# A row-wise top-10 kernel: reordering the extractions, masks and batches of the last tiles

## The chip, the cores and the metric

The kernel runs on one core of a Trainium2 chip. The metric is device time in microseconds (us); the span of a profile is 1.8 us shorter than the time of the same execution (692.61 and 690.8, 690.82 and 689.0). All executions told of here are of the fast state. The engines are called PE (TensorE), VectorE (DVE in the profile), ScalarE (ACT), GpSimd (POOL) and SyncE (SP, which issues the loads). "Pass" is one matmul instruction as the profile counts them: an fp32 matmul shows as two.

## The reference

```python
def setup_inputs():
    return {"x": np.random.randn(8192, 8192).astype(np.float32), "k": 10}

def reference(x, k):
    indices = np.argpartition(x, -k, axis=1)[:, -k:]
    values = np.take_along_axis(x, indices, axis=1)
    sorted_idx = np.argsort(-values, axis=1)
    return np.take_along_axis(indices, sorted_idx, axis=1)
```

## The kernel before

The 8192 rows are 64 tiles of 128 rows. A row is cut into 8 parts, so that a tile holds each row on 8 partitions. Per tile: ScalarE takes steep exponentials; PE sums them over groups of eight columns ("weigh"); VectorE finds the best 16 of the 1024 sums ("choose") and writes the indices of 12 of them; GpSimd gathers the elements behind these ("gather"); VectorE and GpSimd multiply them with a mask, half each ("spread"); PE brings the 96 candidates of each row together in 12 small fp32 matmuls ("extract"); VectorE ranks them ("rank"). Every eight tiles "finish" turns positions into column numbers: seven VectorE steps (slot, low, hot, hot, pick, val, rows), one PE matmul for each tile ("move"), a cast and an output transfer that is issued from ScalarE's queue. Three tiles are loaded ahead.

```python
    starts = list(range(0, ntiles, TB)) + [last - 2, last]      # TB = 8, last = 63
    # ... (cut)
    def spread(t):
        masked[t] = small.tile([P, G, P // 16, 16], fp32, tag="masked", name="masked")
        cand = cands.pop(t)
        half = G // 2                                           # G = 12
        shape = [P, half, P // 16, 16]
        for eng, g0 in ((nc.vector, 0), (nc.gpsimd, half)):
            eng.tensor_tensor(out=masked[t][:, g0:g0 + half], # ... (cut)
                              op=ALU.mult)

    def extract(t):
        mk = masked.pop(t)
        gs[t] = gpsum.tile([P, G, R], fp32, tag="g", name="g")
        for c in range(G):
            nc.tensor.matmul(gs[t][:, c, :], lhsT=mk[:, c, :, :].rearrange("p a s -> p (a s)"),
                             rhs=place, start=True, stop=True)
    # ... (cut)
        for t in range(last):
            interleave(choose_steps(t), rank_steps(t - LAG) if t >= LAG else [])   # LAG = 3
            if t >= 1:
                spread(t - 1)
            gather(t)
            weigh(t + 1)
            if t >= 1:
                extract(t - 1)
            todo = 3 if t < last - 1 else len(later)
            run(later[:todo])                                   # steps of a finished batch
            later = later[todo:]
            # ... (cut: a finished batch appends its finish steps to later; load(t + 3))
        run(choose_steps(last))
        gather(last)
        # ... (cut: a test of the sums, "good")
        spread(last - 1)
        extract(last - 1)
        run(rank_steps(last - 3))
        run(rank_steps(last - 2))
        steps = finish_steps(batch_of[last - 3])
        run(steps[:-2])
        spread(last)
        extract(last)
        run(rank_steps(last - 1))
        run(steps[-2:])
        # ... (cut: finish of tiles 61 and 62, rank of tile 63, finish of tile 63, final test)
```

## Time and profile before

| what | before |
|---|---|
| time, median of all 4 runs known after the prediction | 695.92 us (693.69 to 696.28) |
| profiled execution: time, span | 692.61, 690.8 us |
| loads end | about 645 us |
| last choose starts, its indices are ready | 659.99, 666.46 us |
| last gather ends | 672.28 us |
| last extraction on PE | 679.58 to 682.79 us |

A row of the timeline view gives the start in us, the duration in us, engine, line and operation, the output and inputs, a count, and in brackets how long the engine had been idle and what ended the wait. "issue" there means that nothing in the profile explains the wait. The column after the counts in the view by stretches is the granted share of PE's clock, then the share of the DMA engines and GB/s. One thing in the table will matter below: the profiled execution was faster than any of the four timed ones. The prediction took its durations from that one execution. It was not a freak: of the 41 runs of before in the three groups of experiments below, 12 took under 694 us, 25 over 695.3 and only 4 lie between.

### The profile page before, as it was taken

How to read it: one execution, taken by the hardware profiler on the slowest of the kernel's cores; microseconds unless marked ns; L12 is line 12 of the kernel's file. 1: busy time of each engine (PE TensorE's matmuls, PEld its weight loads, DVE VectorE, ACT ScalarE, POOL GpSimd, SP SyncE). 2: the span in 40 equal slices, each digit the busy share in tenths (PEclk: the TensorE clock that was granted, in tenths of full speed). 3: DMA queues.
4: the chain of work that ended last, by engine and by line, in shares of the span. 5: the costliest groups of instructions: out<-in, count | busy, mean ns of one | idle time of the engine just before them, and what ended most of it. 6: DMA issues, size and time to landing. Idle time of an engine off the chain costs nothing.

```text
span 690.8 us, 7979 instructions
## 1 busy us (share of the span) xinstructions
PE 551.9 (80%) x2690; PEld 340.2 (49%) x2690; DVE 562.6 (81%) x1322; ACT 489.0 (71%) x264; POOL 180.9 (26%) x135
## 2 busy tenths in 40 slices
PE   1587977798898888888987888787987888887835
PEld 0153544464554455555644545554553555654434
DVE  1577787888978997798878898869977897879876
ACT  4777777777777777777777777677777767777700
POOL 0113322322331332232233133313322313332211
PEclk9876688768866688777888698859887677788875
DMA  8999999999999999999999999999999999999300
GB/s 348 421 421 420 419 421 419 421 420 421 419 421 420 419 420 419 421 419 421 420 419 420 419 421 420 420 420 421 415 419 421 420 420 420 421 420 421 140 5 6
DMA packets 70604, 269.69 MB, mean 390 GB/s; under 512 B 4386, under 2 KB 5026, under 8 KB 70562
## 3 DMA queue, kind: packets, MB, share of 16 engines
q1 hardware_dynamic: 69760, 268.45, 94.9%
q10 hardware_dynamic: 802, 0.73, 0.3%
q8 instruction: 21, 0.34, 0.2%
q14 instruction: 21, 0.17, 0.1%
HBM read 268.51 MB, written 0.66 MB: 390 GB/s over the span
## 4 chain that ended last, share of the span: by engine, by line
DMA 56%; PE 12%; DVE 11%; issue 7%; ACT 6%; SPq 5%; POOL 2%; ACTq 0%; POOLq 0%
DMA xt<-in_x_dram 53%; PE s L152 8%; ACT e L144 6%; SPq L94 5%; DMA out_dram<-opack 3%; PE g L212 3%; DVE wall L171 3%; POOL cand L185 2%; DVE m L172 1%; DVE cidb L176 1%; DVE cidb L174 1%; DVE wall L175 1%; DVE masked L201 1%; PE fo L250 1%; DVE pick L267 0%
## 5 line engine op out<-in xcount | busy, mean ns | idle before, releaser
L144 ACT ACTIVATE e<-xt,bias 128x4096 bf16<-128x4096 f32 (+2 forms) x131 | 475.5, 3630 | 157.1 <-DMA xt<-in_x_dram 143.5
L152 PE MATMUL s<-e,group 128*128 128x512 bf16 x1024 | 342.2, 497 | 120.1 <-ACT e L144 119.9
L152 PEld LDWEIGHTS <-group 128*128 128x128 bf16 x1024 | 122.6, 123 | 312.3 <-issue 256.5
L212 PEld LDWEIGHTS g<-cpack,masked 128*128 128x128 f32 x1536 | 208.1, 215 | 29.4 <-issue 15.7
L212 PE MATMUL g<-cpack,masked 128*128 128x8 f32 x1536 | 200.1, 269 | 12.3 <-DVE masked L201 8.5
L185 POOL INDIRECT_COPY cand<-xt,idx 128x192 f32 x64 | 64.5, 1007 | 489.1 <-DVE t8a L223 141.5
L171 DVE MAX8 wall<-s 128x8 f32<-128x1024 f32 x64 | 78.8, 1232 | 113.0 <-PE s L152 112.8
L201 POOL TENSOR_TENSOR masked<-cand,cpack 128x768 f32<-128x768 f32 x64 | 115.5, 1806 | 5.2
L174 DVE FIND_INDEX8 cidb<-wall,s 128x8 uint16<-128x1024 f32 x64 | 78.3, 1223 | 0.0
L176 DVE FIND_INDEX8 cidb<-wall,m 128x8 uint16<-128x1024 f32 x64 | 78.0, 1219 | 0.0
L172 DVE MATCH_REPLACE8 m<-wall,s 128x1024 f32<-128x1024 f32 x64 | 77.7, 1214 | 0.0
L175 DVE MAX8 wall<-m 128x8 f32<-128x1024 f32 x64 | 77.3, 1208 | 0.0
L201 DVE TENSOR_TENSOR masked<-cand,cpack 128x768 f32<-128x768 f32 x64 | 60.7, 949 | 0.0
L250 PE MATMUL fo<-rows,send 128*64 128x160 f32 (+3 forms) x128 | 26.2, 347 | 2.7 <-DVE rows L270 2.7
L144 ACT ACTIVATION_READ_ACCUMULATOR e<-xt,bias 128x1 f32 x131 | 24.4, 186 | 0.0
L330 ACT ACTIVATE e<-tall,bias 128x64 f32<-128x64 f32 x1 | 0.3, 348 | 29.6 <-DVE tall L229 29.6
L250 PEld LDWEIGHTS fo<-rows,send 128*64 128x64 f32 (+3 forms) x128 | 16.8, 146 | 4.5 <-issue 3.0
L223 DVE MAX8 t8a<-g 128x8 f32<-128x96 f32 x64 | 15.9, 248 | 0.8 <-PE g L212 0.8
L226 DVE FIND_INDEX8 posb<-t8a,g 128x8 uint16<-128x96 f32 x64 | 16.4, 256 | 0.0
L228 DVE FIND_INDEX8 posb<-t8b,g 128x8 uint16<-128x96 f32 x64 | 16.1, 252 | 0.0
L224 DVE MATCH_REPLACE8 g<-t8a,g 128x96 f32<-128x96 f32 x64 | 15.9, 248 | 0.0
L227 DVE MAX8 t8b<-g 128x8 f32<-128x96 f32 x64 | 15.5, 243 | 0.0
(37 smaller groups left out, 107.6 us busy)
## 6 DMA issues: line engine op xcount, KB each, us to landing
xt<-in_x_dram SPq DMA_DIRECT2D x248, 1024.0 KB, 16.4
xt<-in_x_dram SPq DMA_DIRECT2D x16, 512.0 KB, 9.5
out_dram<-opack ACTq DMA_DIRECT2D x7, 80.0 KB, 5.2
cpack<-topk_cpack ACTq DMA_DIRECT2D x1, 68.5 KB
out_dram<-opack ACTq DMA_DIRECT2D x1, 50.0 KB
out_dram<-opack ACTq DMA_DIRECT2D x1, 20.0 KB, 1.5
out_dram<-opack ACTq DMA_DIRECT2D x1, 10.0 KB
```

What stands on the lines that cost most here:

```text
L94: nc.sync.dma_start(out=dst[:, s:s + n, :], in_=src[:, s:s + n, :])
L144: nc.scalar.activation(out=e[:, 0:n, :].rearrange("p s j -> p (s j)"), in_=xts[t][:, s0 * W:(s0 + n) * W], func=ACTF.Exp, bias=bias[:, 0:1 ...
L152: nc.tensor.matmul(ss[t][:, j:j + BANK], lhsT=group[:, s0 + i, :], rhs=e[:, i, j:j + BANK], start=s0 + i == 0, stop=s0 + i == S - 1)
L171: lambda: nc.vector.max(out=w16[:, 0:8], in_=m),
L172: lambda: nc.vector.match_replace(out=m2, in_to_replace=w16[:, 0:8], in_values=m, imm_value=-1.0),
L174: lambda: nc.vector.max_index(out=cid[:, 0:8], in_max=w16[:, 0:8], in_values=m),
L175: lambda: nc.vector.max(out=w16[:, 8:16], in_=m2),
L176: lambda: nc.vector.max_index(out=cid[:, 8:16], in_max=w16[:, 8:16], in_values=m2),
L185: nc.gpsimd.add_instruction(mybir.InstIndirectCopy(name=nc.get_next_instruction_name(), ins=[nc.gpsimd.lower_ap(xts[t]), nc.gpsimd.lower_a ...
L201: eng.tensor_tensor(out=masked[t][:, g0:g0 + half], in0=cand[:, g0:g0 + half].unsqueeze(2).to_broadcast(shape), in1=own.rearrange("p (c s) ...
L212: nc.tensor.matmul(gs[t][:, c, :], lhsT=mk[:, c, :, :].rearrange("p a s -> p (a s)"), rhs=place, start=True, stop=True)
L250: nc.tensor.matmul(fo, lhsT=send[:, i, 0:n * S], rhs=rows[:, i].rearrange("p a k -> p (a k)"), start=i == 0, stop=i == n - 1)
```

## The change

Its intent is to shorten the drain behind the last load: the sums of tile 63 go ahead of two extractions on PE, batch 6 (counted from 0: tiles 48 to 55) is finished sooner, the last gather follows tile 62's mask on GpSimd, the last two batches (two tiles and one) become one of three, and the masks of tiles 61 and 63 are divided anew (none and eight of twelve groups on VectorE).

```diff
@@ -78,7 +78,7 @@
 
     last = ntiles - 1
 
-    starts = list(range(0, ntiles, TB)) + [last - 2, last]
+    starts = list(range(0, ntiles, TB)) + [last - 2]
     sizes = [b - a for a, b in zip(starts, starts[1:] + [ntiles])]
     batch_of = {t: b for b, t0 in enumerate(starts) for t in range(t0, t0 + sizes[b])}
 
@@ -192,15 +192,17 @@
         )
         del xts[t], idxs[t]
 
-    def spread(t):
+
+    def spread(t, ndve=G // 2):
         masked[t] = small.tile([P, G, P // 16, 16], fp32, tag="masked", name="masked")
         cand = cands.pop(t)
-        half = G // 2
-        shape = [P, half, P // 16, 16]
-        for eng, g0 in ((nc.vector, 0), (nc.gpsimd, half)):
+        for eng, g0, g1 in ((nc.vector, 0, ndve), (nc.gpsimd, ndve, G)):
+            if g0 == g1:
+                continue
+            shape = [P, g1 - g0, P // 16, 16]
             eng.tensor_tensor(
-                out=masked[t][:, g0:g0 + half],
-                in0=cand[:, g0:g0 + half].unsqueeze(2).to_broadcast(shape),
+                out=masked[t][:, g0:g1],
+                in0=cand[:, g0:g1].unsqueeze(2).to_broadcast(shape),
                 in1=own.rearrange("p (c s) -> p c s", s=16).unsqueeze(1).to_broadcast(shape),
                 op=ALU.mult,
             )
@@ -294,12 +296,12 @@
         for t in range(last):
             interleave(choose_steps(t), rank_steps(t - LAG) if t >= LAG else [])
             if t >= 1:
-                spread(t - 1)
+                spread(t - 1, 0 if t == last - 1 else G // 2)
             gather(t)
             weigh(t + 1)
-            if t >= 1:
+            if 1 <= t < last - 2:
                 extract(t - 1)
-            todo = 3 if t < last - 1 else len(later)
+            todo = 3 if t < last - 4 else 6
             run(later[:todo])
             later = later[todo:]
             done = t - LAG
@@ -307,28 +309,29 @@
                 later += finish_steps(batch_of[done])
             if t + 3 < ntiles:
                 load(t + 3)
+        extract(last - 3)
+        extract(last - 2)
         run(choose_steps(last))
+        spread(last - 1)
         gather(last)
+        extract(last - 1)
+        run(rank_steps(last - 3))
+        run(rank_steps(last - 2))
         nc.vector.tensor_scalar(
             out=good[:, 0:nsums], in0=eall, scalar1=FINITE, scalar2=None, op0=ALU.is_lt,
         )
-        spread(last - 1)
-        extract(last - 1)
-        run(rank_steps(last - 3))
-        run(rank_steps(last - 2))
         steps = finish_steps(batch_of[last - 3])
-        run(steps[:-2])
-        spread(last)
+        run(steps[:3])
+        spread(last, 8)
         extract(last)
+        run(steps[3:7])
         run(rank_steps(last - 1))
+        run(steps[7:-2])
+        run(rank_steps(last))
         run(steps[-2:])
-        steps = finish_steps(batch_of[last - 1])
-        run(steps[:-2])
-        run(rank_steps(last))
 
 
         nc.scalar.activation(out=e10, in_=tall, func=ACTF.Exp, bias=bias[:, 0:1], scale=BETA)
-        run(steps[-2:])
         run(finish_steps(batch_of[last]))
         nc.vector.scalar_tensor_tensor(
             out=good[:, nsums:nsums + ntiles], in0=e10, scalar=SLACK, in1=wall[:, :, G],
```

## The prediction

> **What bounds the kernel now.** I read the page first, its row of DMA shares in particular, then the busy times by stretch, then the chain that ended last from 640 us on, then each engine in order of time in the last 50 us. "Tile 63" is the last of 64; "choose" is the two MAX8/FIND_INDEX8 rounds on a tile's 1024 sums, "weigh" its exponentials and summing matmuls, "spread" the mask product, "extract" the 24 small matmul passes, "rank" the top 10 of 96 candidates, "finish" the assembling and storing of a batch.
>
> ```profile
> DMA 8999999999999999999999999999999999999300
> ...
> 0.00:560.00 560.00, 455.20 (x2194) 276.59 (x2195) 454.62 (x1055) 416.22 (x220) 148.66 (x113) 0.77 1.02 418
> ...
> 650.00:660.00 10.00, 9.63 (x53) 6.24 (x52) 4.96 (x14) 3.15 (x6) 2.59 (x2) 0.85 0.01 2
> 660.00:670.00 10.00, 2.39 (x12) 2.42 (x12) 9.76 (x29) 0.00 (x0) 0.00 (x0) 0.67 0.03 8
> ```
>
> Up to about 645 us the loads fill the queues (share 1.02, 418 GB/s); 268.45 MB at 420 GB/s is 639 us. Nothing in the change touches that stretch before tile 59. What can move is the drain of 690.8 - 645 = 46 us, and there the engines take turns. The start of the drain, in order of time:
>
> ```profile
> 644.53 0.19 ACT L144 ACTIVATION_READ_ACCUMULATOR e<-xt,bias 128x1 f32 x1
> 644.62 1.99 ACT L144 ACTIVATE e<-xt,bias 128x2048 bf16<-128x2048 f32 x1
> ...
> 651.96 1.15 ACT L144 ACTIVATE e<-xt,bias 128x1024 bf16<-128x1024 f32 x1 [1.28 <-issue]
> ...
> 655.20 2.74 PE L212 MATMUL g<-cpack,masked 128*128 128x8 f32 x24
> 657.87 1.84 PE L250 MATMUL fo<-rows,send 128*64 128x160 f32 x12
> ...
> 659.75 0.32 DVE L274 CAST opack<-fo 64x160 uint32<-64x160 f32 x1 [5.04 <-PE fo L250]
> 659.99 1.22 DVE L171 MAX8 wall<-s 128x8 f32<-128x1024 f32 x1
> ```
>
> Tile 63's sums are done at 655.36, yet its choose starts at 659.99: VectorE waits 5.04 us for a copy of batch 6, whose moves (12 passes) queue on PE behind an extraction (24 passes). So 4.6 us are lost to order. The rest:
>
> ```profile
> 666.23 0.23 DVE L177 TENSOR_SCALAR idx<-cidb,cpack 128x12 uint16<-128x12 uint16 x1
> ...
> 671.63 0.65 POOL L185 INDIRECT_COPY cand<-xt,idx 128x192 f32 x1 [12.54 <-issue]
> 672.25 3.55 POOL L201 TENSOR_TENSOR masked<-cand,cpack 128x768 f32<-128x768 f32 x2
> ...
> 672.42 1.70 DVE L268 SCALAR_TENSOR_TENSOR val<-low,pick 128x50 f32<-128x50 uint16 x1
> ...
> 674.15 2.50 DVE L270 TENSOR_TENSOR rows<-val,cpack 128x800 f32<-128x800 f32 x1
> ```
>
> Indices are ready at 666.46, the gather ends at 672.28, GpSimd then makes two half masks (tile 62's waited behind tile 63's gather), and VectorE's two product steps stretch: val ends at 674.12 as the first mask ends at 674.05; rows ends 0.85 us after the second. After that come extract 63 (to 682.8), rank 63 (to 684.3), a cast, finish of a batch of one tile (684.4 to 687.2), and the check (to 688.30); 2.5 us of closing end the span.
>
> **What the skill says.** "SBUF — State Buffer", section "SBUF: two separate sides": GpSimd and a VectorE operation with two SBUF inputs share a port pair, held as an exclusive lock for a whole instruction. The trace agrees: 1.70 and 2.50 us above. The gather too: its record starts 4.29 us after the indices in most tiles, 3.64 in tile 0, which no mask product follows, and 5.24, 4.86 or 5.69 in tiles where a batch's compare, multiply or spreading (1.16, 0.65, 1.48 us, two SBUF inputs each) follows. "TensorE: Matmul & The Clock Gate", section "Architectural detail: the array is 16× 32×32, not 1× 128×128": ScalarE and VectorE are strict FIFO. The trace agrees: at 271 us an exponential waited 2.34 us behind the issue of an output transfer, which waited for VectorE's cast; it began 1.0 us after that cast's start. The same page, section "The HAM clock gate": an idle PE drops to half clock. Here 12 passes took 2.70 us after an idle stretch and 24 took 2.74 when busy.
>
> **The change, part by part.** The order of instructions built from both kernels gives the moves.
>
> (1) Batch 6 is finished earlier: six of its VectorE steps run after tile 59's choose, not three and three. That adds 0.65 + 1.15 + 0.24, about 2.0 us, ahead of choose 60 (now 627.3, was 625.92, where it waited 0.64 anyway). Its spreading (1.48 us) moves ahead of choose 61, which starts 0.7 us late (636.6). Five moves then precede tile 62's sums, three follow them.
>
> (2) The cost that I find in that: the cast and the output issue of batch 6 now stand ahead of tile 63's exponentials on ScalarE (before: behind). Tile 62's sums end at 646.66; three moves are 6 passes, about 1.1 us (12 took 1.84, 4 took 0.89); cast at 647.8; ScalarE free 1.0 us later, at 648.8, not 644.62. Five exponentials with no stall: 3 x 1.99, then 1.24, and 1.29 to the start of the last sums: 657.3; 0.6 for two matmuls: 657.9. VectorE is ready earlier: choose 62 from 648.1, 7.1 us as before (646.69 to 653.79), tile 61's mask no longer on it (0.95 saved): 655.3. So choose 63 starts at 657.9, 2.1 us sooner, not the 4.6 that the removed wait promises.
>
> (3) Choose 63 takes 6.47 us (659.99 to 666.46): 664.4. GpSimd meanwhile makes all of tile 61's mask (2 x 1.8 us, from 649) and half of tile 62's (waits for extract 60, 657.9 + 2.74 = 660.7; done 662.5), so its queue is empty and the gather runs by its lead. Two tiles' ranks, the check of sums and a 0.78 us compare fall into the lead, which then spans 5.5 us to the gather's end (5.82 before with two such products): 670.0, against 672.28.
>
> (4) From gather's end G on. Mask 63 is split 8:4. VectorE 1024 elements: [...]1.22; GpSimd 512: about 1.25 (1.8 for 768). Released together on one lock, they go one after the other: G + 2.5. Then multiply, sum, val, rows: 0.51 + 0.81 + 0.20 + 0.93 = 2.45, G + 4.95 (no GpSimd in the way now). Rank 62: 1.35, G + 6.3. Extract 63: G + 2.5 + 3.2 = G + 5.7, hidden. Rank 63: 1.4, G + 7.7. Ten passes of moves after extract: G + 5.7 + 2.2 = G + 7.9; cast, 0.23. Finish of three tiles: the steps took 1.61 us for one and 2.09 for two, so 2.57: G + 10.7. Six passes and their drain 1.3: G + 12.0. Check 1.4 (686.90 to 688.30), closing 2.5: G + 15.9. Before it was 690.8 - 672.28 = 18.5, so 2.6 saved: two masks at once blocked VectorE, and there was one finish more.
>
> Sum: G falls 2.3, the rest 2.6: 4.9 us, or a span of 685.9. With the runs' 696.25: 691.3.
>
> **Rivals.** (a) ScalarE is not held by the output issue; choose 63 starts at 655.3 and the time is 688.7. For: the engine has idle time there. Against: the 2.34 us at 271 us and FIFO order. (b) The new ScalarE stall, a cold PE in the moves or extractions (2.74 becomes 5.1, as at 596 us) and the lock eat all: each costs 1 to 2.5 us; together 694 to 696. Against: most extractions lie beside choose 63; only extract 63 and the last moves are exposed. (c) The earlier burst on VectorE delays gather 59 by 0.6 us and so the last load. Its transfers queue for 12 to 16 us behind others, so it is hidden; if not, up to 1 us, 692. (d) Mask 63's VectorE part gets the lock first, and extract 63 begins on eight groups while GpSimd works: 0.5 to 1 us better, 690.5.
>
> **Range and chances.** I choose 691.2, between the sum and (d). The range 689.0 to 693.4 takes in (d) and half of (a) below, one cold stretch or a longer ScalarE stall above. Two per cent is 13.9 us, a third of the whole drain; no rival reaches it.
>
> **What would show it.** Right: ScalarE idle about 4 us before the exponentials of tile 63, ended by VectorE's cast; choose 63 near 658; no 5 us wait before the cast; last gather ending near 670; VectorE's and GpSimd's last masks end to end, one of them stretched; three closing batches become two. Wrong: exponentials going on at 644.6; loads ending later than 645; rank 63 waiting long for PE; closing longer than 2.5 us.

## The result, and the profile after

The changed kernel took 690.16 us (689.3 to 690.82), against 695.92 us before: 5.8 us less by the medians. Ratios here are the mean time of one kernel's fast runs over that of the other's of the same rounds, so not quite the ratio of the medians: 0.9923 (95% interval 0.9898 to 0.9948), "same" at the limit of 2%; of 695 us this ratio is about 5.4 us.

By stretches, the kernel after (columns as before):

```profile
DMA  9999999999999999999999999999999999999400
...
0.00:560.00 560.00, 462.11 (x2197) 285.99 (x2198) 454.63 (x1055) 416.70 (x220) 149.19 (x113) 0.76 1.02 418
...
650.00:660.00 10.00, 6.94 (x30) 3.34 (x29) 7.35 (x19) 8.08 (x10) 4.02 (x3) 0.83 0.04 9
660.00:670.00 10.00, 9.54 (x54) 9.44 (x53) 9.61 (x31) 0.00 (x0) 2.51 (x2) 0.59 0.00 0
670.00:680.00 10.00, 9.36 (x42) 8.36 (x41) 7.31 (x23) 0.00 (x0) 2.98 (x2) 0.50 0.01 2
```

The loads run as before. From 660 to 670 us PE is busy for 9.54 us instead of 2.39: the queue of extractions stands there now, beside the last choose. In spite of that its clock is 0.59 and then 0.50.

The start of the drain after, in order of time:

```profile
640.62 2.93 PE L252 MATMUL fo<-rows,send 128*64 128x160 f32 x10
...
643.48 4.27 PE L152 MATMUL s<-e,group 128*128 128x512 bf16 x16
...
644.11 0.19 ACT L144 ACTIVATION_READ_ACCUMULATOR e<-xt,bias 128x1 f32 x1
...
647.68 1.03 PE L252 MATMUL fo<-rows,send 128*64 128x160 f32 x6
...
648.74 0.32 DVE L276 CAST opack<-fo 64x160 uint32<-64x160 f32 x1 [2.86 <-PE fo L252]
...
649.10 0.47 ACTq L278 DMA_DIRECT2D out_dram<-opack  x1
649.75 2.00 ACT L144 ACTIVATE e<-xt,bias 128x2048 bf16<-128x2048 f32 x1 [5.45 <-DVE opack L276]
...
658.13 0.59 PE L152 MATMUL s<-e,group 128*128 128x512 bf16 x2 [0.54 <-ACT e L144]
...
658.76 1.23 DVE L171 MAX8 wall<-s 128x8 f32<-128x1024 f32 x1 [2.64 <-PE s L152]
```

The wait before the cast has shrunk from 5.04 to 2.86 us and no longer stands in front of the last choose. ScalarE, which had gone straight on at 644.62, now stands still for 5.45 us until the cast. The cast waits for PE, which works without a pause here: five moves of batch 6 (2.93 us, at a clock of 0.52 from 640 to 645 us), tile 62's sums to 647.75, the last three moves. So the last choose starts only 1.2 us sooner than in the profile before (658.76 for 659.99).

Around the last gather, after:

```profile
665.09 0.23 DVE L177 TENSOR_SCALAR idx<-cidb,cpack 128x12 uint16<-128x12 uint16 x1
...
670.08 0.68 POOL L185 INDIRECT_COPY cand<-xt,idx 128x192 f32 x1 [6.83 <-DVE hot L263]
...
670.79 1.23 DVE L203 TENSOR_TENSOR masked<-cand,cpack 128x1024 f32<-128x1024 f32 x1 [0.88 <-POOL cand L185]
670.84 2.29 POOL L203 TENSOR_TENSOR masked<-cand,cpack 128x512 f32<-128x512 f32 x1
671.94 1.53 DVE L266 TENSOR_TENSOR hot<-hot,cidb 128x600 f16<-128x600 f16 x1
...
672.17 5.26 PE L214 MATMUL g<-cpack,masked 128*128 128x8 f32 x24 [0.65 <-DVE masked L203]
677.36 2.89 PE L252 MATMUL fo<-rows,send 128*40 128x160 f32 x10
```

VectorE had the port pair first (1.23 us, unhindered), GpSimd's third (four groups of twelve) took 2.29 us instead of some 1.2, and VectorE's next product waited for it in turn (1.53 us for a step that took 0.47 before). The extraction behind took 5.26 us where the profile before has 3.21.

### The profile page after: what moved, and what is told of

Same layout as the page of the kernel before. It is cut to its first block, busy times and chain, and to the rows that moved or that the text cites. A ratio compares the mean times of both kernels' runs of the same rounds, so it can differ in the third digit from the quotient of the medians.

```text
span 689.0 us, 7967 instructions
## 1 busy us (share of the span) xinstructions
PE 566.8 (82%) x2690; PEld 354.3 (51%) x2690; DVE 558.5 (81%) x1313; ACT 488.8 (71%) x264; POOL 183.1 (27%) x135
## 5 line engine op out<-in xcount | busy, mean ns | idle before, releaser
L214 PEld LDWEIGHTS g<-cpack,masked 128*128 128x128 f32 x1536 | 221.3, 227 | 21.7 <-DVE masked L203 7.2
L214 PE MATMUL g<-cpack,masked 128*128 128x8 f32 x1536 | 213.0, 278 | 4.6 <-DVE masked L203 4.6
L203 POOL TENSOR_TENSOR masked<-cand,cpack 128x768 f32<-128x768 f32 x64 | 117.7, 1839 | 6.0 <-PE g L214 0.7
L203 DVE TENSOR_TENSOR masked<-cand,cpack 128x768 f32<-128x768 f32 (+1 forms) x63 | 60.0, 952 | 0.9 <-POOL cand L185 0.9
L252 PE MATMUL fo<-rows,send 128*64 128x160 f32 (+2 forms) x128 | 28.7, 373 | 3.0 <-DVE rows L272 3.0
L252 PEld LDWEIGHTS fo<-rows,send 128*64 128x64 f32 (+2 forms) x128 | 18.2, 158 | 6.0 <-issue 3.9
```

The source lines that it names most:

```text
L203: eng.tensor_tensor(out=masked[t][:, g0:g1], in0=cand[:, g0:g1].unsqueeze(2).to_broadcast(shape), in1=own.rearrange("p (c s) -> p c s", s= ...
L252: nc.tensor.matmul(fo, lhsT=send[:, i, 0:n * S], rhs=rows[:, i].rearrange("p a k -> p (a k)"), start=i == 0, stop=i == n - 1)
```

## The experiments

The gather's instruction was not allowed in experiments. So all twelve runs carry a stand-in that is wrong on purpose, and the last test is turned so that the quick path ends the kernel; every result is wrong, the launch, the outputs and all other instructions are those of the kernel named. The stand-in, on GpSimd:

```diff
-        nc.gpsimd.add_instruction(mybir.InstIndirectCopy(...))   # cut
+        nc.gpsimd.tensor_copy(out=fill[:, 0:G], in_=idxs[t])
+        for _ in range(6):
+            nc.gpsimd.memset(fill, 0.0)                          # 128 x 576 words
+        nc.gpsimd.tensor_copy(out=cands[t].rearrange("p g s -> p (g s)"),
+                              in_=xts[t][:, 0:16 * G])
...
-            op0=ALU.mult, op1=ALU.is_gt,                         # the last test
+            op0=ALU.mult, op1=ALU.is_le,
```

The medians of before in the three groups of runs were 695.73 (e1 to e4), 695.7 (e5 to e8) and 695.6 us (e9 to e12), so medians may be compared across groups within some tenths.

| run | time, us | ratio to before |
|---|---|---|
| e1 before, stand-in | 695.2 (692.51 to 698.07) | 1.0004 |
| e2 after, stand-in | 689.61 (689.01 to 690.57) | 0.9934 |
| e3 output issue late | 686.33 (686.06 to 687.24) | 0.9885 |
| e4 18 idle matmuls | 689.34 (688.83 to 689.77) | 0.9929 |
| e5 extractions in the loop | 691.9 (690.89 to 692.75) | 0.9945 |
| e6 gather first | 692.06 (691.79 to 693.41) | 0.995 |
| e7 two batches | 690.91 (690.64 to 694.09) | 0.9942 |
| e8 e3 with 33 idle matmuls | 684.71 (683.88 to 690.09) | 0.9873 |
| e9 batch 6 by threes | 686.91 (686.64 to 686.94) | 0.9886 |
| e10 e3, cast late | 686.05 (683.85 to 688.68) | 0.9867 |
| e11 e8, cast late, 45 idle matmuls | 684.59 (683.41 to 684.86) | 0.9846 |
| e12 e11, mask on VectorE alone | 686.46 (685.05 to 689.2) | 0.9886 |

### e1 and e2: does the stand-in keep the effect?

> The kernel before with its gather replaced, because the gather's instruction is not allowed in experiments: a small copy of the indices, six fills of 576 words and a copy of 192 words of the tile, sized to last as long as the gather (4.65 us from the indices to the end); candidates and results are wrong on purpose, and the final test is turned so that the quick path ends the kernel. If the stand-in is good, the time lies within 2 us of before's 695.9 (ratio 0.997 to 1.003). Theory 1 (the profiled run of before was a lucky one, in which PE warmed up near the end: its span was 690.8 where 694 is usual): this profile shows a span of 693 to 695 with the extraction of the last tile at about 5.2 us. Rival (the load phase varies by 3 us from run to run): the last load lands later than 645 us in slow executions and the last extraction may be short.

> The changed kernel with the same stand-in. If the stand-in keeps what matters, its time is 5 to 6.5 us under that of e1 (ratio to before 0.990 to 0.994); ScalarE waits some 5 us before the last tile's exponentials, and the last choose starts at about 658.8 us. If the gain came from the gather's own behaviour with the port pair, the difference of e1 and e2 is under 3 us.

It does: 695.2 and 689.61 us, 5.6 us apart, where the real pair is 5.8 apart. So the gain does not hang on the gather's own way with the port pair. In e1 PE's last extraction, as the timeline has it:

```profile
679.91 5.29 PE L212 MATMUL g<-cpack,masked 128*128 128x8 f32 x24
```

The granted clock was 0.50 there. In the profile before, the same 24 passes and the clock:

```profile
679.58 3.21 PE L212 MATMUL g<-cpack,masked 128*128 128x8 f32 x24
```

```profile
680.00:685.00 5.00, 3.44 (x27) 3.01 (x27) 3.94 (x22) 0.35 (x1) 0.00 (x0) 0.84 0.03 10
```

From the start of this extraction to the end e1 took 693.2 - 679.91 = 13.3 us and the profile before 690.8 - 679.58 = 11.2. The profile that the prediction was read from was a lucky one: PE's clock rose just in time (0.84 from 680 to 685 us). What let it rise is not shown: in both profiles PE had been busy without a pause with the same moves and passes since 677 us. The rise accounts for 2.1 us of the 3 by which it undercuts the usual run; what scatters before's runs between 692 and 698 us otherwise was not looked into.

In e2 the timeline shows PE without a pause:

```profile
657.60 18.56 PE L214 MATMUL g<-cpack,masked 128*128 128x8 f32 x96
```

All 96 passes of four extractions stand in one row, 0.19 us each. Of busy time there is no lack, and yet the clock, 0.84 from 655 to 660 us, is at 0.50 from there on:

```profile
660.00:665.00 5.00, 5.00 (x25) 5.00 (x25) 4.86 (x8) 0.00 (x0) 2.37 (x2) 0.50 0.00 0
```

### e3: the output issue behind the last exponentials

> e2 with one thing undone: the issue of batch 6's output transfer stands behind the last tile's exponentials again; the cast stays where it is. Theory (the FIFO wait of ScalarE for that cast costs on the path): the exponentials go on at 644.2, the last choose starts at about 656.1 when VectorE is done with the one before it, 2.6 us sooner, and the time is 2 to 2.6 us under e2. Rival (the wait lies beside VectorE's work and costs nothing): within 0.7 us of e2.

```diff
-            todo = 3 if t < last - 4 else 6
+            todo = 3 if t < last - 4 else 4 if t == last - 2 else 6
```

686.33 us, 3.3 under e2: more than the 2 to 2.6 expected. The timeline shows the exponentials going on at once and the last choose following VectorE's last step:

```profile
645.24 1.99 ACT L146 ACTIVATE e<-xt,bias 128x2048 bf16<-128x2048 f32 x1
...
655.55 1.22 DVE L173 MAX8 wall<-s 128x8 f32<-128x1024 f32 x1
```

So ScalarE's wait of 4 to 5 us is a real cost of the change. It is one transfer issue of 0.47 us, at the wrong place in a queue that keeps its order. The last choose came 2.2 us sooner than in e2's profile, and the two profiled executions are just as far apart (689.49 and 687.24); the further 1 us by which the medians differ is not assigned.

### e4 and e8: the clock of PE

> e2 with 18 matmuls of 128x512 without use among the extractions of tiles 60, 61 and 62 (one behind every fourth pass). Theory (the small extraction passes do not count as activity for TensorE's clock, which drops to half from 661 us on, and the last extraction and the moves are exposed): granted clock above 0.8 from 660 to 675, the last extraction takes under 3.5 us instead of 5.3, the moves under 2.3 instead of 2.9, and the time is 2 to 4 us under e2. Rival (the clock is low for another reason, or other work hides the extraction): within 0.7 us of e2, or slower by the 18 matmuls.

```diff
             nc.tensor.matmul(gs[t][:, c, :], ...)
+            if warm is not None and c % 2 == 1:        # extractions 60, 61, 62
+                nc.tensor.matmul(warm[:, 0:BANK], lhsT=group[:, 0, :],
+                                 rhs=...,  # 512 columns of group
+                                 start=True, stop=True)
```

(The added matmuls are called idle: nobody uses their result.) 689.34 us, 0.3 under e2: the expectation of 2 to 4 us fell. By stretches, then the last extraction from the timeline:

```profile
660.00:665.00 5.00, 4.40 (x39) 3.93 (x37) 4.82 (x9) 0.00 (x0) 2.84 (x3) 1.00 0.00 0
665.00:670.00 5.00, 5.00 (x29) 4.61 (x29) 4.33 (x21) 0.00 (x0) 4.63 (x8) 0.59 0.01 3
```

```profile
670.49 5.15 PE L214 MATMUL g<-cpack,masked 128*128 128x8 f32 x24
```

The clock held at 1.00 to 665 us (0.50 in e2) and fell before the extraction that counts, while idle matmuls still ran among tile 62's passes. So e4 tells that such matmuls hold the clock up for a while, and nothing about what a fast last extraction is worth. e8 put more of them in, on top of e3.

> e3 with more matmuls without use than e4: one of 128x512 behind every two groups in extractions 60 and 61, nine after them to fill PE's idle time, and one behind every group of extraction 62. Theory (the clock falls because small passes leave the array idle; e4's matmuls were too few, as the clock held till 666 us and then fell): clock above 0.8 up to 670 us, extraction 63 under 3.5 us instead of 5.26, moves under 2.2 instead of 2.89, and the time 1.5 to 3.5 us under e3. Rival 1 (the clock falls for another reason): clock 0.5 from 665 on and the time that of e3 or worse. Rival 2 (the clock holds, but VectorE's steps set the end): extraction short, time within 0.7 us of e3.

```diff
+        extract(last - 3, 2)      # one idle matmul behind every 2 groups
+        extract(last - 2, 2)
+        burn(9)                   # nine more, while PE waits for mask 62
...
+        extract(last - 1, 1)      # one behind every group
```

Four of six runs lie between 683.88 and 684.74 us; the median, 684.71, is 1.6 under e3 (the mean of all six only 0.2). Two runs took 690.0 and 690.1 at a lower mean clock (0.765 for 0.773 to 0.789), were not profiled, and stay unexplained. By stretches and in the timeline:

```profile
665.00:670.00 5.00, 3.81 (x34) 3.45 (x32) 4.62 (x9) 0.00 (x0) 3.38 (x4) 1.00 0.00 0
```

```profile
667.55 2.82 PE L222 MATMUL g<-cpack,masked 128*128 128x8 f32 x24 [1.19 <-DVE masked L203]
```

The extraction took 2.82 us instead of 5.26. The moves behind stayed slow (2.89): the clock had fallen by then. So the half clock costs the changed kernel 2.4 us on the last extraction, of which 1.6 shows in the median time; e11, which has no such slow runs, lies 1.5 us under e10 with idle matmuls added in the same way. And e2's row of 96 passes of 8 columns did not hold the clock up.

### e5: the extractions back in the loop

> e2 with the first part of the change undone: the extractions of tiles 60 and 61 stand inside the loop again, ahead of the sums of tiles 63 and behind them as before. Theory (the three moves before the cast then queue behind an extraction of 2.74 us, the cast, ScalarE and the last choose come that much later): ScalarE's wait before the last exponentials is about 6.7 us instead of 3.9, the last choose starts near 660.5, and the time is 1.7 to 3 us over e2. Rival (the order of the extractions is of no worth, because extraction 60 leaves PE's full queue at the end): within 0.7 us of e2.

```diff
-            if 1 <= t < last - 2:
+            if t >= 1:
                 extract(t - 1)
...
-        extract(last - 3)
-        extract(last - 2)
```

691.9 us, 2.3 over e2, as expected: this part is worth it. The cast in the timeline:

```profile
651.76 0.32 DVE L276 CAST opack<-fo 64x160 uint32<-64x160 f32 x1 [5.46 <-PE fo L252]
```

Its wait is 5.46 us (1.98 in e2), the last choose starts at 661.77 instead of 657.79.

### e6: the gather ahead of mask 62

> e2 with the last gather ahead of tile 62's mask again on GpSimd. Theory: GpSimd's half of mask 62 moves from beside the last choose to behind the gather, 1.8 us, mask 63's quarter follows it, and VectorE's products are locked out meanwhile; the second half of extraction 62 and extraction 63 come later; 2 to 3 us over e2. Rival (the mask was hidden either way): within 0.7 us of e2.

```diff
-        spread(last - 1)
         gather(last)
+        spread(last - 1)
```

692.06 us, 2.45 over e2, as expected. In the timeline VectorE's mask of tile 63 waits for GpSimd's half of tile 62's, and the extraction behind:

```profile
670.45 2.80 DVE L203 TENSOR_TENSOR masked<-cand,cpack 128x1024 f32<-128x1024 f32 x1 [0.57 <-POOL cand L190]
```

That is 2.80 us for a step that takes 1.23 alone.

### e7: two batches at the end

> e2 with the last batch of three tiles cut into two and one again. Theory from the steps' lengths (finish of two 2.33 with its cast, then the rank of tile 63 1.4 that was hidden behind the moves, then a finish of one 1.84 and its moves 0.9, against 2.79 + 1.98): 1.2 to 2.2 us over e2. Rival (the extra batch hides behind PE's slow matmuls): within 0.7 us of e2.

```diff
-    starts = list(range(0, ntiles, TB)) + [last - 2]
+    starts = list(range(0, ntiles, TB)) + [last - 2, last]
...
+        steps = finish_steps(batch_of[last - 1])
+        run(steps[:-2])
         run(rank_steps(last))
-        run(steps[-2:])
```

(The first batch's cast runs before these lines, the second's behind the exponential of the tenth values.) 690.91 us (five runs within 0.4, one at 694.09, unexplained), 1.3 over e2, at the lower edge of what was expected: merging the batches is worth a little over a microsecond.

### e9: batch 6 finished three steps at a time

> e2 with another part undone: batch 6 is finished three steps at a time as before, its cast and output issue behind the last tile's sums. Theory (with the extractions out of the way, the early finish is not needed and its output issue only holds ScalarE): exponentials of the last tile go on at 644; six moves stand between the last sums and the cast; the last choose starts 2 us behind the last sums, near 656.3 (e3: right after VectorE is free, 655.6; e2: 657.8); 1 to 2.5 us under e2's 689.6. Rival (the early finish is what removed the 5 us wait): the wait before the cast is back and the time is 2 us or more over e2.

```diff
-            todo = 3 if t < last - 4 else 6
+            todo = 3 if t < last - 1 else len(later)
```

686.91 us, 2.7 under e2, a little more than expected. With this part of the change undone the kernel is faster. In the timeline the cast waits for nothing on record and the last choose follows:

```profile
654.91 0.30 DVE L276 CAST opack<-fo 64x160 uint32<-64x160 f32 x1
655.14 1.21 DVE L173 MAX8 wall<-s 128x8 f32<-128x1024 f32 x1
```

With the extractions out of the way the six moves that stand ahead of the cast take 1.84 us; little was left for the early finish to remove. What costs is the place of its output issue: e3, which keeps the early finish and moves only the issue, lies 0.6 us under e9.

### e10, e11 and e12: looking for a faster version

> e3 with the cast of the batch before last moved behind the seven VectorE steps of the last batch's finish. Theory (those steps wait in line for ten passes on PE that they do not need: 1.38 us of waiting and 0.3 of cast): 1 to 1.8 us under e3's 686.3. Rival (the last moves wait for the cast instead, nothing gained): within 0.5 us of e3.

```diff
         run(rank_steps(last))
+        ending = finish_steps(batch_of[last])
+        run(ending[:7])
         run(steps[-2:])
...
-        run(finish_steps(batch_of[last]))
+        run(ending[7:])
```

686.05 us, 0.3 under e3, with runs from 683.85 to 688.68: in the times this is inconclusive. From the end of the last rank to the end of the last VectorE step the profile shows 6.1 us (678.2 to 684.31) where e3's has 7.5 (675.39 to 682.92), the 1.4 us that were expected. The profiled run itself was the slowest of the five; an extraction at 638 us took 5.13 us at a low clock in it and held up the cast of batch 6 until 651.03 (648.26 in e3). The early finish makes the drain depend on PE's clock before the last load, too; e9, without it, varied by 0.3 us only. (This is a reading of one profile and of five runs each.)

> e8 with the late cast, and twelve more matmuls without use where PE has nothing else to do: three behind the last extraction, nine behind the moves of the batch before last. Theory: ten moves under 2 us instead of 2.89, the last six about 1 us instead of 1.2; the cast wait of e8 is only 0.28, so little is left there; 0.5 to 1.5 us under e8's 684.7. Rival (the added matmuls delay the moves): e8 or worse.

(Edit: e8 and e10 together, with three more idle matmuls behind the last extraction and nine behind the moves.) 684.59 us, 0.1 under e8, less than expected by the medians, though without e8's two slow runs. The ten moves took 2.62 us in its profile, not the expected 2; the last six 1.00. It is the fastest of all, 11 us under before (ratio 0.9846, 95% interval 0.9827 to 0.9865) and 5.0 under e2. With the real gather it was not run, so this is shown for the stand-in only.

> e11 with the whole of the last tile's mask on VectorE and none on GpSimd. Theory (both parts run one after the other on the shared port pair, 1.15 + 1.1 us, against one instruction of 1.75 us): the product that follows takes 0.47 instead of 1.53, VectorE reaches its rows 0.5 us sooner, and the time is 0.2 to 0.6 us under e11, perhaps lost in the scatter. Rival (the two parts overlap): the mask alone takes longer than both and the time is 0.5 us over e11.

```diff
-        spread(last, 8)
+        spread(last, G)
```

686.46 us, 1.9 over e11: a miss. VectorE did as expected, the product behind the mask took 0.47 us again; but in the timeline of PE:

```profile
669.04 4.02 PE L222 MATMUL g<-cpack,masked 128*128 128x8 f32 x24 [1.73 <-DVE masked L203]
```

PE waits 1.73 us for the whole mask (1.18 in e11 for the first eight groups), its clock falls in the middle, and the extraction takes 4.02 us instead of 2.82. The nine idle matmuls then stand in front of the last moves, which began 1.7 us after the cast that released them. That the longer pause made the clock fall is the likely reading, but was not tested by itself.

## Why the prediction was right

The time (691.2 predicted, 690.16 measured) and the gain (4.9 to 5.1 and 5.8) came out well. Step by step, against the profile after:

- **Part 1, batch 6 early.** VectorE's two delays came as worked out (choose 61 starts 9.3 us after choose 60, at 637.88). VectorE was 1.2 us later than in the profile before already at tile 59's indices (624.04 for 622.84).
- **Part 2, the cost on ScalarE.** Predicted: a wait of 4.2 us and the last choose at 657.9. Measured: 5.45 us and 658.76. The mechanism was right, and e3 shows that it costs time; its term was too small. The prediction left the end of tile 62's sums where it was (646.66), as if the five moves ahead of them cost nothing; they took 2.93 us, the extraction before them 4.07 (2.74 in the profile before), and the sums ended at 647.75. Rival (a) falls.
- **Part 3, the gather.** Predicted 5.5 us from indices to the gather's end, measured 665.32 to 670.76 = 5.44. Two more leads fit the reading with the port lock: 3.64 us for tile 62, which no VectorE product with two SBUF inputs follows, as for tile 0 before; and 5.69 for tile 60, behind whose indices rows stands. The stand-in shows such waiting without a gather: in e2 its first small copy took 0.19 us where no such product ran, 0.91 beside a mask and 2.31 beside a mask and rows. e6 confirms that the mask's place on GpSimd matters. The gather ended 1.5 us sooner than in the profile before, not 2.3.
- **Part 4, from the gather's end.** Masks end to end: right. VectorE's part was put at 1.22 us and took 1.23; it went first, as rival (d) has it, and extraction 63 did begin on the eight groups, at 672.17, before GpSimd was done at 673.13. Rows at 4.95 us after the gather, measured 4.8. Then the sizes go wrong: "Extract 63: G + 2.5 + 3.2" took 5.26, "ten passes of moves" 2.89 instead of 2.2, the last six 1.77 and not the 1.3 with drain. So the end came 18.2 us after the gather, not 15.9.
- **Why the sum held all the same.** From profile to profile the change saved only 690.8 - 689.0 = 1.8 us: 1.5 up to the gather's end (2.3 predicted) and 0.3 behind it (2.6 predicted). The 3.2 us was taken from the one profile of before, where PE's clock happened to rise, and all parts from a run that was 3.6 us faster than the 696.25 from which the saving was taken off. The step that failed is this mixing: the span was predicted at 685.9 and measured at 687.5 to 689.0. The pair e1 and e2 compares like with like, with the last extraction at half clock in both: there the stand-in for the last gather ended at 672.63 and 669.49, 3.1 us sooner, and from there to the end it took 20.6 and 18.2 us, 2.4 less. So the error stands on both sides and nearly cancels in the difference. The prediction did not argue that it would; to that extent its close hit is luck.
- **Rivals (b) and (c).** A PE at half clock did take 2 to 3 us, as (b) said it could, but before has it too in its usual run, if e1's profile stands for that. (c): the last load still ended at about 645 us.

What each part is worth in the changed kernel, by undoing it: the order of the extractions 2.3 us (e5), the gather behind the mask 2.45 (e6), one batch 1.3 (e7), and the early finish of batch 6 with its output issue minus 2.7 (e9). The parts need not add up. The new division of the masks was not undone by itself in the changed kernel; of tile 63's only e12 says something, under other conditions.

## What to carry to other kernels

Behind the last load each engine worked through its list in order here (ScalarE in e3, PE in e5): look, for each item moved forward, which other item it now stands in front of, transfer issues included, since 0.47 us of issue cost 2 to 3 us here by waiting for a cast. Take durations of PE from more than one execution when the clock is not the same in each, and never mix a profile's durations with the median of other runs without comparing the two. Once one wait is removed, try the change without the parts that were meant for the same wait.

## What the Trainium skill lacked or had wrong

- "TensorE: Matmul & The Clock Gate", section "The HAM clock gate": says that some 3.4 us of sustained activity raise the clock, and little of what counts as activity. In e2 PE was busy for 18.56 us with 128x8 fp32 passes and was granted 0.50 from 660 us on. With a 512-column matmul behind every second pass pair (e4) it held 1.00 up to 665 us and fell while the same mix went on; with more of them (e8) it held until 670 us. That many-column matmuls are needed is not shown: in the profile before, the clock rose to 0.84 (680 to 685 us) without any.
- The same page, on the drop: it names an idle window of about 3.4 us. In e12 the last extraction took 4.02 us after a pause of 1.73, against 2.82 after 1.18 in e11. That short pauses beside small passes suffice is a reading of these two, not tested by itself.
- "GPSIMD Engine Reference" has no duration for a gather from SBUF by a list in SBUF. Here, for 192 elements per group of partitions, the record of 1.01 us begins 3.64 us after the indices if VectorE leaves the port pair alone. "Perfetto Trace Analysis", section "GPSIMD Engine Instruction", fits: it has the record begin at the first tensor read, not at the instruction's start.
- "SBUF — State Buffer", section "SBUF: two separate sides", calls the loser of the port pair fully blocked; the trace after agrees (2.29 us for GpSimd's third, 1.53 for a VectorE product of 0.47). That a gather gives way too, as the leads of 3.64 to 5.69 us suggest, is within its rule; no page gives these leads.
